# Attention by pairs of heads, and the values product in three rounded parts, in a hybrid layer on one Trainium2 core

## Chip, core and metric

One Trainium2 chip, one core. The metric is the device time of the kernel in microseconds: 351.48 us is the median of three runs before (351.43 to 351.65).

## The reference

A layer for 256 tokens of width 1024 with two branches whose outputs are gated and added. The part that the change touches is the attention branch: eight heads of 128, causal softmax with a relative bias over one block of 256 keys, then the product of probabilities and values, a gate by silu, and a projection.

```python
logit_own = jnp.einsum('bhqd,bhjd->bhqj', qc, k_own) * scale + bias_own
logit_own = jnp.where(dist_own >= 0, logit_own, NEG_INF)
p = jax.nn.softmax(jnp.concatenate([logit_sel, logit_own], axis=-1), axis=-1)
...
o = (jnp.einsum('bhqkj,bhqkjd->bhqd', p_sel, v_sel)
     + jnp.einsum('bhqj,bhjd->bhqd', p_own, v_own))
...
ya = (ya * jax.nn.silu(za)) @ w_att_proj
```

With 256 tokens there is one block, so `sel` contributes nothing. The other branch is an mLSTM of four heads of 256; its input and forget gates (`ig`, `fg`) go through a log-sigmoid, a running sum and a running maximum, and give factors that scale its scores. Everything is float32.

## The kernel before

After a first phase (normalisation and the q and k projections) the kernel runs through 23 chunks of weights, in order: three of values `va` (344 columns), then two halves each of `za`, `qm`, `km`, `att`, `zm`, `vm`, `om`, `ga`, `gm`, `ml`, `out`. Each chunk is four groups of two weight tiles, so there are 92 groups, numbered from 0. A group of `za`, `qm`, `km`, `att` (groups 12 to 43) is 24 matmuls of 256 columns (lines 1006, 1008 and 1009), and its result lies in PSUM until the chunk's four groups are done.

Each weight is used as two rounded parts in TensorE's one-pass float type (F32R in the code): ACT casts the weight to `wh` (line 448), DVE or, for eight groups from 27 on, POOL subtracts to get `wl` (line 452), and TensorE makes three products, high with high, high with low and low with high. These halves are made four groups ahead (`split(g + 4)`, five buffers), so ACT's cast for group g + 4 waits until TensorE has finished group g - 1.

Everything else is hung on group numbers by hand. `at(g, fn)` runs a piece of work in group g after the cast and subtraction; `between(g, fn)` runs it between the cast and the subtraction. On TensorE both come ahead of group g's own matmuls, so what TensorE does there is a burst of small matmuls between two groups. Each engine works its instructions in this order.

Attention before: for head h, in group 10 + h TensorE makes the scores (`att_qk`, lines 604 and 605) and DVE moves them out with the bias; ACT takes the exponential in the same group (`att_exp`); DVE normalises one group later (`att_norm`); TensorE transposes three groups later (`att_PT`, lines 629 to 631) and ACT copies the result to `PT`. `att_av` takes two heads at a time, in groups 18, 20, 21 and 22: per head one plain float32 product of 256 columns (line 642, keys 0 to 127 for all queries) and one of 128 columns (line 644, keys 128 to 255 for the later queries). DVE multiplies with silu(za), ACT and POOL split the result into `yah` and `yal` (lines 649 and 650), which the projection reads from group 36 on.

The gate factors run beside this: `gates_3` to `gates_7`, `gates_T` and `gates_D` at groups 12 to 21. `gates_5` (group 17) ends with ACT making the tile `GE` (line 565) and SP writing a row to memory (line 567); `gates_T` (group 18) transposes `GE` on TensorE (line 587). Tiles that are not in use at the same time share a place (`slot`): `G`, the gate tile, has the place "s6", the bias the place "bias", which the conditioning vector `cbg` takes over in `gate_init` (line 828).

Of the kernel before, what the change touches and what calls it, by code (L numbers as in the profile page):

```python
# [9 lines left out]
F32 = mybir.dt.float32  # L10
F32R = mybir.dt.float32r
AF = mybir.ActivationFunctionType
OP = mybir.AluOpType
# [5 lines left out]
AH, AD = 8, 128  # L19
# [47 lines left out]
def tile_hybrid(ctx: ExitStack, tc: tile.TileContext, x, c, params2, w_row, w_va, ada_mod, ada_gate,  # L67
                w_in, w_att_proj, w_ml_proj, w_out, out):
    nc = tc.nc
# [163 lines left out]
    for j in range(4):  # L233
        n, q = divmod(j, 2)
        nc.tensor.matmul(pc[:, n, q * 256:(q + 1) * 256], pick[:, j:j + 1].to_broadcast([128, 128]), cparts,
                         start=q == 0, stop=q == 1, skip_group_check=True)
# [66 lines left out]
    for step in P1_STEPS:  # L303
        op, k = step[0], int(step[1])
        if op == "L":
            next_loads(k)
        else:
# [4 lines left out]
                 v=lambda k: split_low(k, nc.vector, 1024, NR), g=lambda k: split_low(k, nc.vector, 1024, 1536),  # L312
                 h=lambda k: split_low(k, nc.vector, 1536, NR), G=modulate_low,
                 c=lambda k: modulation_sum(k, 1), k=lambda k: modulation_sum(k, 0),
                 a=modulation_scale, b=modulation_shift, i=lambda k: modulate(k, "i"), j=lambda k: modulate(k, "j"),
                 P=lambda k: mm_row(k, 0), Q=lambda k: mm_row(k, 1, (0, 1)), q=lambda k: mm_row(k, 1, (2,)),
# [28 lines left out]
    C = {}  # L345
# [3 lines left out]
    def done(name, half):  # L349
        return 4 * (C[name, half] + 1)  # L350
# [76 lines left out]
    def slot(tag, shape, dt, name):  # L427
        free(tag)
        return hl.tile(shape, dt, name=name, tag=tag, bufs=1)

    def aux(shape):
        return ps.tile(shape, F32, name="aux", bufs=4)
# [24 lines left out]
    def at(step, fn, *a):  # L457
        hooks.setdefault(step, []).append((fn, a))

    def between(step, fn, *a):  # L460
        hooks_between.setdefault(step, []).append((fn, a))

    T = {}
# [162 lines left out]
    def att_PT(h):  # L626
# [4 lines left out]
        nc.tensor.transpose(pa[:, 256:384], P[:, 128:256], ident)  # L631
        nc.scalar.copy(T["PT"][:, h], pa)

    def att_av(h0):
        va, PT, sza = T["va"], T["PT"], T["za"]
        if "yah" not in T:
            T["yah"] = slot("s1", [128, AH, S], F32R, "yah")
            T["yal"] = slot("s2", [128, AH, S], F32R, "yal")
        pa = aux([128, 2, 256])
        for hh in range(2):  # L640
            h = h0 + hh
            nc.tensor.matmul(pa[:, hh, :], va[:, 0, h * 128:(h + 1) * 128], PT[:, h, 0:256], start=hh == 0,  # L642
                             stop=False, skip_group_check=True)
            nc.tensor.matmul(pa[:, hh, 128:256], va[:, 1, h * 128:(h + 1) * 128], PT[:, h, 256:384], start=False,
                             stop=hh == 1, skip_group_check=True)
        yf = hl.tile([128, 2, 256], F32, name="yf", tag="scr", bufs=2)
        hs = slice(h0, h0 + 2)
        nc.vector.tensor_tensor(yf, pa, sza[:, hs], op=OP.mult)
        nc.scalar.copy(T["yah"][:, hs], yf)
        nc.gpsimd.tensor_tensor(T["yal"][:, hs], yf, T["yah"][:, hs].bitcast(F32), op=OP.subtract)  # L650
# [232 lines left out]
    at(10, gates_2)  # L883
    at(12, qk_T, "k", 1)
    A0 = 10
    for h in range(AH):
        between(A0 + 1 + h, att_norm, h)
        between(A0 + h, att_qk, h)
        hooks_between.setdefault(A0 + 3 + h, []).insert(0, (att_PT, (h,)))
        at(A0 + h, att_exp, h)  # L890
    for step, fn in ((12, gates_3), (14, gates_copy), (15, gates_4), (17, gates_5), (18, gates_6), (18, gates_T),
                     (19, gates_7), (21, gates_D)):
        at(step, fn)
    for nm in ("qm", "km"):
        for hf in range(2):
            s = done(nm, hf)
            for q in range(2):
                at(s + q, lambda i, *a: conv(mmt[i], *a), C[nm, hf], hf, nm, q)
                at(s + q + 1, conv_silu, hf, nm, q)
    for q in range(2):  # L900
        at(done("za", 0) + 2 + 2 * q, att_av, 2 * q)
        at(done("za", 1) + 1 + q, att_av, 4 + 2 * q)
    s = 4 * C["zm", 0]
    for half in range(2):
        at(s + 5 * half, ml_split, half)
        at(s + 5 * half + 3, ml_scores, 2 * half)
        at(s + 5 * half + 4, ml_scores, 2 * half + 1)
    at(4 * C["att", 0] - 10, gate_init)
    gate_left = {}
    for q, nm in enumerate(GSEG):  # L910
        s = 4 * C[nm, 0] - 4
# [164 lines left out]
```

## Time and profile before

| | |
|---|---|
| median of three runs | 351.48 us |
| profiled execution | 351.84 us, its span 350.0 us |
| TensorE (PE) | 344.3 us busy, 98% of the span |
| DVE, ACT, POOL | 247.0, 213.3 and 87.8 us busy |
| granted TensorE clock | 1.000 |
| groups 12 to 27 (attention, most of it) | 83.56 to 139.25 us of the span |

PE is TensorE, PEld its weight loads, DVE the vector engine, ACT the scalar engine, POOL GpSimd, SP the engine that issues most DMAs. A row of a timeline gives start, length, engine, line, operation and what is written and read; in brackets stands how long the engine was idle before and what ended that. A matmul in plain float32 shows as two records. Durations of matmul records overlap, so what one costs is read from start to start, or from the chain of waits, whose pieces do not overlap.

### The profile page before, as it was taken

What the parts mean: (1) busy time and instruction counts of PE and PEld (TensorE: products, weight loads), DVE (VectorE), ACT (ScalarE), POOL (GpSimd) and SP (SyncE); (2) the same over time, 40 slices, a digit from 0 to 9 for tenths busy, and PEclk for the clock granted to TensorE, in tenths of its full rate; (3) what the DMA queues carried; (4) which work ended last, traced back from release to release, by engine and by line L of the source; (5) the groups of instructions that cost most, each with busy time, mean ns of one, the idle gap of its engine ahead of it and who ended that gap; (6) DMA issues with size and microseconds to landing.
All of it is one profiled execution on the core that took longest, in us unless ns stands there. A gap on an engine that the chain in (4) does not pass through costs nothing.

```text
span 350.0 us, 6175 instructions
## 1 busy us (share of the span) xinstructions
PE 344.3 (98%) x2432; PEld 323.1 (92%) x2432; DVE 247.0 (71%) x369; ACT 213.3 (61%) x331; POOL 87.8 (25%) x81
## 2 busy tenths in 40 slices
PE   8999999999999999999999999999999999999996
PEld 7788889999999999999998888888899999999995
DVE  4999996976994437768866693864475775469961
ACT  4768779799777867675646554445646374543510
POOL 4400002942202462555004352000010320452000
PEclk9999999999999999999999999999999999999999
DMA  7999999890671554493874837659119129291011
GB/s 286 416 413 416 415 419 418 223 385 13 197 285 62 161 200 134 151 375 125 322 279 151 330 120 245 237 163 388 51 29 381 72 70 367 107 292 69 2 62 60
DMA packets 23517, 77.79 MB, mean 222 GB/s; under 512 B 3001, under 2 KB 4929, under 8 KB 22849
## 3 DMA queue, kind: packets, MB, share of 16 engines
q1 hardware_dynamic: 23336, 76.87, 59.9%
q10 hardware_dynamic: 152, 0.53, 0.5%
q8 instruction: 19, 0.31, 0.3%
q14 instruction: 10, 0.07, 0.1%
HBM read 76.14 MB, written 1.25 MB: 221 GB/s over the span
## 4 chain that ended last, share of the span: by engine, by line
PE 96%; DMA 2%; DVE 1%; issue 0%; SPq 0%; ACT 0%; DVEq 0%; ACTq 0%
PE mm L1009 15%; PE mm L1006 15%; PE mm L1008 15%; PE pm L198 13%; PE mm L999 8%; PE mm L1000 8%; PE mm L1001 8%; PE mm L992 3%; DMA adat<-in_ada_mod_dram 2%; PE mm L1021 1%; PE aux L642 1%; PE mm L1020 1%; PE mm L1019 1%; PE aux L492 1%; PE aux L604 1%; PE aux L762 1%
## 5 line engine op out<-in xcount | busy, mean ns | idle before, releaser
L452 DVE TENSOR_TENSOR wl<-raw,wh 128x1024 fp32r<-128x1024 f32 (+1 forms) x92 | 118.7, 1302 | 64.1 <-ACT wh L448 64.1
L448 ACT CAST wh<-raw 128x1024 fp32r<-128x1024 f32 (+1 forms) x100 | 100.5, 1015 | 54.2 <-PE mm L1001 26.7
L1006 PE MATMUL mm<-hTh,wh 128*128 128x256 f32 x320 | 90.0, 281 | 0.0
L1008 PE MATMUL mm<-hTl,wh 128*128 128x256 f32 x320 | 88.7, 277 | 0.0
L1009 PE MATMUL mm<-hTh,wl 128*128 128x256 f32 x320 | 88.7, 277 | 0.0
L1006 PEld LDWEIGHTS mm<-hTh,wh 128*128 128x128 f32 x320 | 60.2, 188 | 0.0
L1008 PEld LDWEIGHTS mm<-hTl,wh 128*128 128x128 f32 x320 | 60.2, 188 | 0.0
L1009 PEld LDWEIGHTS mm<-hTh,wl 128*128 128x128 f32 x320 | 60.1, 188 | 0.0
L999 PE MATMUL mm<-wh,hTh 128*128 128x512 f32 (+1 forms) x144 | 53.0, 368 | 0.0
L1000 PE MATMUL mm<-wl,hTh 128*128 128x512 f32 (+1 forms) x144 | 52.6, 365 | 0.0
L1001 PE MATMUL mm<-wh,hTl 128*128 128x512 f32 (+1 forms) x144 | 52.6, 365 | 0.0
L1001 PEld LDWEIGHTS mm<-wh,hTl 128*128 128x128 f32 x144 | 27.0, 188 | 3.8
L999 PEld LDWEIGHTS mm<-wh,hTh 128*128 128x128 f32 x144 | 27.0, 188 | 3.6
L1000 PEld LDWEIGHTS mm<-wl,hTh 128*128 128x128 f32 x144 | 27.1, 188 | 3.5
L452 POOL TENSOR_TENSOR wl<-raw,wh 128x1024 fp32r<-128x1024 f32 x8 | 19.5, 2461 | 18.4 <-ACT wh L448 12.1
L183 ACT CAST wrh<-raw 128x512 fp32r<-128x512 f32 (+1 forms) x24 | 18.2, 761 | 8.0 <-DMA raw<-in_w_row_dram 7.9
L188 DVE TENSOR_TENSOR wrl<-raw,wrh 128x512 fp32r<-128x512 f32 (+1 forms) x26 | 20.3, 807 | 0.5 <-ACT wrh L183 0.5
L198 PE MATMUL pm<-wrh,hTh 128*128 128x512 f32 x64 | 19.9, 392 | 0.8 <-ACT hTh L168 0.8
L198 PE MATMUL pm<-wrh,hTl 128*128 128x512 f32 x64 | 19.8, 391 | 0.0
L198 PE MATMUL pm<-wrl,hTh 128*128 128x512 f32 x64 | 18.7, 391 | 0.0
L1009 PE MATMUL mm<-yah,wl 128*128 128x256 f32 x64 | 17.7, 276 | 0.0
L1006 PE MATMUL mm<-yah,wh 128*128 128x256 f32 x64 | 17.7, 276 | 0.0
(218 smaller groups left out, 659.3 us busy)
## 6 DMA issues: line engine op xcount, KB each, us to landing
raw<-in_w_in_dram SPq DMA_DIRECT2D x32, 1024.0 KB, 5.2
adat<-in_ada_mod_dram SPq DMA_DIRECT2D x16, 512.0 KB, 8.8
raw<-in_w_va_dram SPq DMA_DIRECT2D x6, 688.0 KB, 9.2
raw<-in_ada_gate_dram SPq DMA_DIRECT2D x4, 1024.0 KB, 6.8
raw<-in_w_att_proj_dram SPq DMA_DIRECT2D x4, 1024.0 KB, 4.8
raw<-in_w_ml_proj_dram SPq DMA_DIRECT2D x4, 1024.0 KB, 6.3
raw<-in_w_out_dram SPq DMA_DIRECT2D x4, 1024.0 KB, 6.3
raw<-in_w_row_dram SPq DMA_DIRECT2D x15, 256.0 KB, 8.1
```

Source lines behind the costliest of these rows:

```text
L183: copy(wsp[k][0][:, c0:c1], wrow[k][:, c0:c1])
L188: e.tensor_tensor(l[:, cs], wrow[k][:, cs], h[:, cs].bitcast(F32), op=OP.subtract)
L198: nc.tensor.matmul(pm[ch][:, t], a[:, k, t * 128:(t + 1) * 128], b[:, cs], start=k == 0 and i == 0, stop=k == KT - 1 and i == 2)
L448: nc.scalar.copy(h, w)
L452: e.tensor_tensor(l, w, h.bitcast(F32), op=OP.subtract)
L992: nc.tensor.matmul(mmt[ci][:, t, cs], a, w[:, kk, cs], start=first and i == 0 and c0 == 0 and w is wh, stop=last and i == 1 and c0 > 0, sk ...
L999: nc.tensor.matmul(o, a, wh[:, kk], start=first, stop=False)
L1000: nc.tensor.matmul(o, a, wl[:, kk], start=False, stop=False)
L1001: nc.tensor.matmul(o, b, wh[:, kk], start=False, stop=last)
L1006: nc.tensor.matmul(o, wh[:, kk, cs], sh_[:, k], start=first and i % 2 == 0, stop=False, skip_group_check=True)
L1008: nc.tensor.matmul(o, wh[:, kk, cs], sl_[:, k], start=False, stop=False, skip_group_check=True)
L1009: nc.tensor.matmul(o, wl[:, kk, cs], sh_[:, k], start=False, stop=last and i % 2 == 1, skip_group_check=True)
```

## The change

Three things, in the order of the code.

1. `att_av` is made of three rounded products per head instead of one plain one for the 256-column part. A new function `av_split` makes the parts for two heads: ACT casts the values of the two heads (`vh`, 128x256) and their transposed probabilities (`PTs`, 128x512) and POOL subtracts to get the lower parts. It runs in groups 18 and 20 for the first four heads and in 23 and 24 for the last four. `att_av` then runs for four heads in group 23 and for four in group 27 (before: two each in 18, 20, 21 and 22). The 128-column part stays plain. `PTs` lies in the place of `G` for the first four heads and in that of the bias for the last four; `vh` and `vl` take the places of `P`.
2. Attention runs by pairs of heads: scores of two heads in groups 10, 12, 14 and 16, normalisation of both one group later, transposes of both four groups later (14, 16, 18, 20).
3. `gates_5` moves from group 17 to 16, and `gate_init` from group 26 to 28.

```diff
+    def av_split(h0):
+        if h0 % 4 == 0:
+            T["PTs", h0] = slot("bias" if h0 else "s6", [128, 2, 2, 2, 256], F32R, "PTs")
+        p = T["PTs", h0 // 4 * 4][:, h0 // 2 % 2]
+        vh, vl = (hl.tile([128, 256], F32R, name=nm, tag="P", bufs=4) for nm in ("vh", "vl"))
+        T["vs", h0] = vh, vl
+        for h, l, src in ((vh, vl, T["va"][:, 0, h0 * 128:h0 * 128 + 256]), (p[:, 0], p[:, 1], T["PT"][:, h0:h0 + 2, 0:256])):
+            nc.scalar.copy(h, src)
+            nc.gpsimd.tensor_tensor(l, src, h.bitcast(F32), op=OP.subtract)
+
     def att_av(h0):
...
         pa = aux([128, 2, 256])
+        ps_, (vh, vl) = T["PTs", h0 // 4 * 4][:, h0 // 2 % 2], T["vs", h0]
         for hh in range(2):
             h = h0 + hh
-            nc.tensor.matmul(pa[:, hh, :], va[:, 0, h * 128:(h + 1) * 128], PT[:, h, 0:256], start=hh == 0,
+            nc.tensor.matmul(pa[:, hh, 128:256], va[:, 1, h * 128:(h + 1) * 128], PT[:, h, 256:384], start=hh == 0,
                              stop=False, skip_group_check=True)
-            nc.tensor.matmul(pa[:, hh, 128:256], va[:, 1, h * 128:(h + 1) * 128], PT[:, h, 256:384], start=False,
-                             stop=hh == 1, skip_group_check=True)
+        for hh in range(2):
+            c = slice(hh * 128, hh * 128 + 128)
+            for i, (v, p) in enumerate(((vh, 0), (vh, 1), (vl, 0))):
+                nc.tensor.matmul(pa[:, hh, :], v[:, c], ps_[:, p, hh], start=False, stop=hh == 1 and i == 2,
+                                 skip_group_check=True)
...
     A0 = 10
-    for h in range(AH):
-        between(A0 + 1 + h, att_norm, h)
-        between(A0 + h, att_qk, h)
-        hooks_between.setdefault(A0 + 3 + h, []).insert(0, (att_PT, (h,)))
-        at(A0 + h, att_exp, h)
-    for step, fn in ((12, gates_3), (14, gates_copy), (15, gates_4), (17, gates_5), (18, gates_6), (18, gates_T),
+    for h in range(0, AH, 2):
+        for fn, d in ((att_PT, 4), (att_qk, 0), (att_norm, 1)):
+            for hh in (h, h + 1):
+                between(A0 + h + d, fn, hh)
+        for hh in (h, h + 1):
+            at(A0 + h, att_exp, hh)
+    for i in range(A0 + 4, A0 + AH + 4, 2):
+        hooks_between[i].sort(key=lambda f: f[0] is not att_PT)
+    for step, fn in ((12, gates_3), (14, gates_copy), (15, gates_4), (16, gates_5), (18, gates_6), (18, gates_T),
                      (19, gates_7), (21, gates_D)):
         at(step, fn)
...
-    for q in range(2):
-        at(done("za", 0) + 2 + 2 * q, att_av, 2 * q)
-        at(done("za", 1) + 1 + q, att_av, 4 + 2 * q)
+    s = done("za", 1)
+    for q0, av, splits in ((0, 3, (-2, 0)), (2, 7, (3, 4))):
+        for q in range(2):
+            at(s + splits[q], av_split, 2 * (q0 + q))
+        for q in range(2):
+            at(s + av, att_av, 2 * (q0 + q))
...
-    at(4 * C["att", 0] - 10, gate_init)
+    at(4 * C["att", 0] - 8, gate_init)
```

What this does to the order of instructions is seen at two places. The first is TensorE's burst with the values product for two heads (`aux` is its PSUM tile, `vat` the values). Before, ahead of group 21:

```order
L1009 MATMUL mm<-hTh,wl 128x256
L642 MATMUL aux<-PT,vat 128x256
L644 MATMUL aux<-PT,vat 128x128
L642 MATMUL aux<-PT,vat 128x256
L644 MATMUL aux<-PT,vat 128x128
L1006 MATMUL mm<-hTh,wh 128x256
```

Now, the first of two such pieces that stand ahead of group 23:

```order
L1029 MATMUL mm<-hTh,wl 128x256
L653 MATMUL aux<-PT,vat 128x128 x2
L658 MATMUL aux<-PTs,vh 128x256 x2
L658 MATMUL aux<-PTs,vl 128x256
L658 MATMUL aux<-PTs,vh 128x256 x2
L658 MATMUL aux<-PTs,vl 128x256
L653 MATMUL aux<-PT,vat 128x128 x2
```

Two plain products of 256 columns are gone and six rounded ones stand in their place, behind the two plain ones of 128 columns; the last row begins the next two heads in the same burst.

The second place is POOL's queue from the gate tile (`NM` is the decay tile, made from the gate factors) to the weight halves of `qm`. Before:

```order
L650 TENSOR_TENSOR yal<-yf,yah 128x512
L578 COPY NM<-NM 128x4x128
L581 AFFINE_SELECT NM<-NM 128x4x128 x2
L650 TENSOR_TENSOR yal<-yf,yah 128x512 x3
L452 TENSOR_TENSOR wl<-raw,wh 128x1024 x8
```

Now:

```order
L642 TENSOR_TENSOR vl<-vat,vh 128x256
L642 TENSOR_TENSOR PTs<-PT,PTs 128x512
L452 TENSOR_TENSOR wl<-raw,wh 128x1024
L664 TENSOR_TENSOR yal<-yf,yah 128x512 x2
L642 TENSOR_TENSOR vl<-vat,vh 128x256
L642 TENSOR_TENSOR PTs<-PT,PTs 128x512
L452 TENSOR_TENSOR wl<-raw,wh 128x1024
L642 TENSOR_TENSOR vl<-vat,vh 128x256
L642 TENSOR_TENSOR PTs<-PT,PTs 128x512
L452 TENSOR_TENSOR wl<-raw,wh 128x1024
L664 TENSOR_TENSOR yal<-yf,yah 128x512 x2
L452 TENSOR_TENSOR wl<-raw,wh 128x1024 x5
```

These rows begin with the second of the four splits. The lower halves of groups 27 and 28 now stand ahead of and between the last two splits, and the four parts of `yal` come in two pairs.

## The prediction

> **What bounds the kernel now.** First the page of the profile: busy time by engine, and the shares of the chain that ended last.
>
> ```profile
> span 350.0 us, 6175 instructions
> PE 344.3 (98%) x2432; PEld 323.1 (92%) x2432; DVE 247.0 (71%) x369; ACT 213.3 (61%) x331; POOL 87.8 (25%) x81
> PE 96%; DMA 2%; DVE 1%; issue 0%; SPq 0%; ACT 0%; DVEq 0%; ACTq 0%
> ```
>
> TensorE is busy for 98% of the span and makes up 96% of the chain. So what counts is TensorE's own issue time, plus any wait that appears in it. Work on ACT, DVE and POOL costs nothing until TensorE has to wait for it. Next the chain in order of time, which gives real issue steps (the durations of matmul records overlap). Columns: start, length in us, what.
>
> ```profile
> 105.69 0.24 PE aux L587 x2
> 105.93 0.63 PE aux L642 x2
> ...
> 114.67 0.22 PE aux L644 x2
> ...
> 117.72 0.43 PE aux L642 x2
> ...
> 118.37 0.43 PE aux L642 x2
> ...
> 118.80 0.22 PE aux L644 x2
> ...
> 121.76 0.43 PE aux L642 x2
> ```
>
> Read three things here. One plain float32 product of values with 256 columns (L642) takes 0.43 us, the 128-column one (L644) 0.22 us. After the burst that ends at 118.80 + 0.22 = 119.02 us, the 24 weight matmuls of a group last until 121.76: 2.74 us. After the burst that ends at 114.67 + 0.22 = 114.89 us, the same work lasts until 117.72: 2.83 us. So TensorE has two paces. The timeline shows both without any burst in between:
>
> ```profile
> 83.56 0.36 PE L1006 MATMUL mm<-hTh,wh 128*128 128x256 f32 x1
> 139.25 0.28 PE L1006 MATMUL mm<-hTh,wh 128*128 128x256 f32 x1
> 271.98 0.28 PE L1006 MATMUL mm<-hTh,wh 128*128 128x256 f32 x1
> 274.80 0.28 PE L1006 MATMUL mm<-hTh,wh 128*128 128x256 f32 x1
> 283.99 0.28 PE L1006 MATMUL mm<-hTh,wh 128*128 128x256 f32 x1
> 286.70 0.28 PE L1006 MATMUL mm<-hTh,wh 128*128 128x256 f32 x1
> ```
>
> Rows 3 to 6 are the starts of neighbouring groups of 24 matmuls: 2.82 us apart in the one place (0.118 each), 2.71 to 2.72 us in the other (0.113 each). Rows 1 and 2 are the starts of groups 12 and 28, which enclose most of the attention: 55.69 us.
>
> **The change part by part.** (a) The product. For each of the eight heads a 0.43 us matmul goes and three rounded ones of the same 256 columns come; the 0.22 us matmul stays. The trace has such rounded products inside a burst, in the mLSTM scores:
>
> ```profile
> 191.56 0.72 PE aux L762 x6
> ```
>
> Six in 0.72 us is 0.120 each; in the weight groups they cost 0.113. Three cost 0.34 to 0.36 us, so a head saves 0.07 to 0.09 us and eight heads 0.56 to 0.74 us. I take 0.65.
>
> (b) The gate factors. In group 18's burst TensorE transposes the tile GE, which ACT has only just made:
>
> ```profile
> PEld aux L587 <- ACT GE L565: 0.2, 1, 0.2
> 105.05 0.42 ACT L565 ACTIVATE GE<-G 4x256 f32<-4x256 f32 x1 [0.89 <-DVE st L622]
> 105.31 0.27 PE L630 MATMUL aux<-ident,P 128*128 128x128 f32 x1
> 105.42 0.27 PE L631 MATMUL aux<-ident,P 128*128 128x128 f32 x1
> 105.62 0.31 PE L587 MATMUL aux<-ident,GE 36*128 36x36 f32 x2
> ```
>
> L630 to L631 is 0.11 us, L631 to L587 0.20: 0.09 lost. The product right behind took 0.63 instead of 0.43 (the chain above), another 0.20, which I can't split into wait and refill. With the factors made in group 16, some 3.7 us sooner, GE is long there. Gain between 0.1 and 0.3; I take 0.25.
>
> (c) Fewer bursts. Attention work stood between the groups fifteen times from group 7 to 22; in pairs it stands there ten times (before groups 7, 8, 10, 12, 14, 16, 18, 20, 23, 27). A burst followed by the quick pace costs 2.74 - 2.72 = 0.02 us, one followed by the slow pace 2.83 - 2.72 = 0.11. Five fewer: 0.1 to 0.55; I take 0.1 and treat the pace by itself.
>
> A ceiling follows from groups 12 to 28: 16 groups x 2.72 = 43.52, five score pairs and eight value pairs of 0.65 = 8.45, 24 transposes x 0.11 = 2.64, gate transposes 0.24, together 54.85 of the 55.69 us. So some 0.85 us of waits, refills and slow pace lie in this stretch, and the change can gain at most 0.74 + 0.85 = 1.6 us.
>
> (d) The splits on ACT and POOL. ACT gets four casts of 128x256 and four of 128x512, POOL four subtractions of each size. Nearest rows:
>
> ```profile
> L452 POOL TENSOR_TENSOR wl<-raw,wh 128x1024 fp32r<-128x1024 f32 x8 | 19.5, 2461 | 18.4 <-ACT wh L448 12.1 <-PE mm L1009 6.3
> L650 POOL TENSOR_TENSOR yal<-yf,yah 128x512 fp32r<-128x512 f32 x4 | 5.2, 1306 | 27.4 <-ACT yah L649 27.4
> L750 POOL TENSOR_TENSOR qms<-qmT,qms x2: 2392/2884/3377, 186.7 to 202.4; 128x1024 fp32r<-128x1024 f32 x2
> L448 ACT CAST wh<-raw 128x1024 fp32r<-128x1024 f32 x88 | 91.4, 1048 | 51.6 <-PE mm L1001 24.2 <-PE mm L1008 21.1 <-issue 1.5
> L632 ACT COPY PT<-aux 128x384 f32<-128x384 f32 x8 | 3.8, 474 | 0.0
> L649 ACT CAST yah<-yf 128x512 fp32r<-128x512 f32 x4 | 2.5, 616 | 4.9 <-DVE yf L648 4.9
> ```
>
> Per pair of heads ACT works 0.35 + 0.62 = about 1 us more, POOL 0.7 + 1.31 = 2.0 us (0.35 and 0.7 are estimates for 256 columns, from the 0.47 of 384 on ACT and from half of 1.31 on POOL). ACT writes a weight group's upper half four groups (11 us) ahead, so 1 us is covered; the cover ends where POOL must finish before TensorE reads. The tight place is the second half. Count from t0, when group 22 ends. ACT comes late, since in group 21 it loads a table and makes the decay tile:
>
> ```profile
> 118.75 1.28 ACT L595 ACT_TABLE_LOAD   x1
> ...
> 122.54 0.39 ACT L596 ACTIVATE NM<-NM,gc 128x128 f32<-128x128 f32 x1
> ```
>
> That is 4.2 us behind a 1.0 us cast that waits for group 20's end (t0 - 5.4); two more casts end at about t0 + 1.7. Then POOL has, in order: group 27's lower half 2.46, two lower halves of the attention output 2 x 1.31, one value and probability split 2.0, group 28's lower half 2.46, the last split 2.0: 11.5 us, done at t0 + 13.2. TensorE comes to the last lower half after two products (2 x 1.1), four groups (10.9), one product (1.1) and three matmuls (0.55): t0 + 14.8. Slack 1.6 us; no wait. The first half is easier: its splits start in groups 18 and 20 and are read at 23. What is queued on POOL behind the last split is group 31's lower half, needed four groups later. ACT's DMA of the conditioning vector moves two groups back, behind the last products; it landed 3.7 us after issue at 138.4, and its first reader starts at 154.6:
>
> ```profile
> L828 ACTq DMA_DIRECT2D cbg<-in_c_dram x1: 365/365/365, 138.4 to 138.4; - x1
> DMA to landing us min/median/max: 3.7/3.7/3.7
> L832 DVE CUSTOM_DVE_ANT_0 raw<-raw,cbg,prm x8: 1274/1279/2321, 154.6 to 226.1; 128x1024 f32<-128x1024 f32 x8
> ```
>
> Two groups (5.4 us) later is still over 7 us early. SP issues the factors' small write one group sooner, past the weight loads of that group only; ACT's first probability cast waits for that write, made some 5 us before. Both at nothing.
>
> Sum: 0.65 + 0.25 + 0.1 = 1.0 us. The profiled execution took 351.84 us (span 350.0 and 1.84 around it), 0.36 above the median of 351.48. Off its own time that is 350.8; the terms are issue times that every execution pays, so I take them off the median: **350.5 us**.
>
> **The rivals.** *The slow pace catches on behind the last burst (slower).* The pace after a burst stays as it is until something disturbs it: in the rows at 271.98 and 274.80 it stayed slow over a border between groups with no burst there. Before, the last attention burst stood ahead of group 22 and happened to be followed by the quick pace. Now the last stands ahead of group 27, with another form of matmul at its end, and 17 groups of 24 follow before the shape changes at group 44. If it catches there, it costs 17 x 0.11 = 1.8 us, and the time is 350.5 + 1.8 = 352.3. It turns to slower than before from 10 of these groups on (1.0 / 0.107). For it: of the two bursts of products quoted first, one went slow and one quick. Against: over the whole trace slow is the rarer one, about one burst in three, and a single disturbance ends it. Chance 0.22.
>
> *POOL is late for the last split.* A POOL subtraction of 1024 elements has taken 2.39 to 3.38 us here. At 3.38, with the others stretched by the same 1.4, the 11.5 us become 16 and TensorE waits up to 3.0 us; at the 2.88 median of that row they become 13.5, a wait of 0.4 us. What stretches them is DVE working beside POOL:
>
> ```profile
> 89.49 0.73 POOL L544 TENSOR_TENSOR G<-G 4x256 f32<-4x256 f32 x1 [8.53 <-ACT wh L448]
> 89.57 0.80 DVE L623 TENSOR_SCALAR P<-P,st 128x256 f32<-128x256 f32 x1
> 93.01 0.35 DVE L623 TENSOR_SCALAR P<-P,st 128x256 f32<-128x256 f32 x1
> 123.51 1.31 POOL L650 TENSOR_TENSOR yal<-yf,yah 128x512 fp32r<-128x512 f32 x1 [4.87 <-ACT yah L649]
> 124.42 1.49 DVE L452 TENSOR_TENSOR wl<-raw,wh 128x1024 fp32r<-128x1024 f32 x1 [3.83 <-ACT wh L448]
> ...
> L452 DVE TENSOR_TENSOR wl<-raw,wh x92: 861/1224/3408, 50.4 to 334.3; 128x1024 fp32r<-128x1024 f32 x80, 128x688 fp32r<-128x688 f32 x12
> ```
>
> The same DVE instruction takes 0.35 us alone and 0.80 beside POOL, and one with two inputs 1.49 against a median of 1.22; POOL's own kept its 1.31. So DVE mostly pays, and POOL's 1.6 us of slack should hold. If POOL were held for the whole of each of the two DVE subtractions of groups 29 and 30 (1.22 each), it would come 0.8 us late: 351.3. Chance of a late POOL 0.13, at 350.9 to 351.3 and seldom more. The Trainium skill, page "SBUF — State Buffer", section "SBUF: two separate sides", says that the port pair which DVE and GpSimd share is an exclusive lock, the loser blocked for the whole instruction; that is the 351.3 case, and it speaks against moving work to POOL. The first two rows above agree with it (DVE as the loser), the last two only in part: 1.49 us is less than the 0.40 us left of POOL's instruction plus a full 1.22.
>
> *Only the product counts.* The bursts become longer and the pace after the short ones (groups 12 to 26, 15 groups) may be slow in half of them: 7 x 0.107 = 0.75 us given back, or GE's gap is a refill that stays. Time 350.9 to 351.3. For it: three short stretches were slow before. Chance 0.17.
>
> **How the numbers follow.** Chances: forecast 0.48 (350.0 to 351.0), product only 0.17, late POOL 0.13, slow pace 0.22. The range reaches from the ceiling, 351.48 - 1.6 = 349.9, to the slow pace held throughout, 352.3. A measurement of this kernel can tell about 0.2% (0.7 us) from no change: faster is under 350.8, slower over 352.2. Faster takes nearly all of the forecast and some of the product-only case: 0.52. Slower is two thirds of the slow pace and a POOL worse than bounded: 0.17. Same is the rest: 0.31.
>
> **What would show it.** Right: three rounded products in 0.34 to 0.36 us in place of 0.43; no gap ahead of the gate transposes; ten bursts; groups 28 to 43 at 2.72 us. Wrong: groups 28 to 43 at 2.82; TensorE idle ahead of the last products with POOL as what ended it; a new wait of TensorE for ACT or DVE in groups 12 to 22, where the pairs ask two tiles of each at once.

## The result and the profile after

The changed kernel takes 353.61 us (median of four runs, 352.92 to 354.01), the kernel before 351.46 us beside it (351.32 to 351.65). The ratio is 1.006, 95% interval 1.0044 to 1.0076: slower by some 2 us. The forecast was 350.5 us with a range up to 352.3, so both the sign and the range were wrong.

The page of the changed kernel: span, busy time by engine, share of the chain that ended last.

```profile
span 351.6 us, 6213 instructions
PE 345.9 (98%) x2440; PEld 324.1 (92%) x2440; DVE 248.7 (71%) x369; ACT 216.8 (62%) x339; POOL 101.0 (29%) x89
PE 98%; ACT 1%; POOL 0%; DVE 0%; issue 0%; POOLq 0%
```

The profiled execution took 353.35 us. The span grew by 1.6 us, and so did TensorE's busy time (344.3 to 345.9), although TensorE has less to do than before. It is not waiting for a neighbour: DVE and POOL are 0% of the chain, and ACT's 1% lies in its first 7 us. Its own instructions take longer. The timeline shows where (first matmuls of groups 7, 28, 29, 30 and 44):

```profile
69.34 0.40 PE L1019 MATMUL mm<-wh,hTh 128*128 128x344 f32 x1
...
139.09 0.28 PE L1026 MATMUL mm<-hTh,wh 128*128 128x256 f32 x1
...
141.92 0.28 PE L1026 MATMUL mm<-hTh,wh 128*128 128x256 f32 x1
...
144.75 0.28 PE L1026 MATMUL mm<-hTh,wh 128*128 128x256 f32 x1
...
184.32 0.40 PE L1019 MATMUL mm<-wh,hTh 128*128 128x512 f32 x1
```

Groups 28 and 29 take 2.83 us each, with no burst between them, and groups 28 to 43 together 45.23 us: 16 x 2.827. Before, the same 16 groups took 43.52 us: 16 x 2.72, from 139.25 to 182.77. The starts of groups 7 and 44 in the timeline of the kernel before:

```profile
69.52 0.40 PE L999 MATMUL mm<-wh,hTh 128*128 128x344 f32 x1
...
182.77 0.40 PE L999 MATMUL mm<-wh,hTh 128*128 128x512 f32 x1
```

The difference is 1.71 us, more than the whole growth of the span, in a place where the change adds nothing to TensorE. In the records TensorE is in the slow pace (0.1178 us from matmul to matmul in place of 0.1133) from group 18 without a break to group 43, in 26 groups. Before, only groups 12, 13 and 20 of those from 12 to 43 were slow. 26 x 0.107 is 2.8 us.

The products themselves went as forecast. Chain of waits of the changed kernel, start, length, what; L653 are the plain 128-column products, L658 the rounded ones:

```profile
120.50 0.45 PE aux L653 x4
120.94 0.71 PE aux L658 x6
...
135.28 0.44 PE aux L653 x4
135.72 0.71 PE aux L658 x6
```

Six rounded products in 0.71 us are 0.118 each; three replace a plain one of 0.43, so a head saves 0.08 and eight heads 0.62 us. POOL was in time too: in its timeline the last split (L642) ends at 132.99 + 1.30 = 134.29 us, and TensorE's first product that can read it starts at 135.72. The rows also show a split before it, and DVE's subtraction beside the last one:

```profile
126.98 0.75 POOL L642 TENSOR_TENSOR vl<-vat,vh 128x256 fp32r<-128x256 f32 x1
...
128.95 2.39 POOL L452 TENSOR_TENSOR wl<-raw,wh 128x1024 fp32r<-128x1024 f32 x1
...
129.95 2.47 DVE L452 TENSOR_TENSOR wl<-raw,wh 128x1024 fp32r<-128x1024 f32 x1
...
131.30 1.73 POOL L642 TENSOR_TENSOR vl<-vat,vh 128x256 fp32r<-128x256 f32 x1
132.99 1.30 POOL L642 TENSOR_TENSOR PTs<-PT,PTs 128x512 fp32r<-128x512 f32 x1
```

The gate transposes did not get cheaper. In the timeline the factors `GE` are ready at 104.05 + 0.42 = 104.47, half a microsecond ahead of the last attention transpose, and yet the step from L631 to L587 is 0.21 us, as before:

```profile
104.05 0.42 ACT L565 ACTIVATE GE<-G 4x256 f32<-4x256 f32 x1 [0.56 <-DVE st L622]
...
104.98 0.27 PE L631 MATMUL aux<-ident,P 128*128 128x128 f32 x1
105.19 0.31 PE L587 MATMUL aux<-ident,GE 36*128 36x36 f32 x2
105.42 0.39 PE L1026 MATMUL mm<-hTh,wh 128*128 128x256 f32 x1
```

The waits of TensorE's weight loads put these 0.2 us to no engine ("issue"), where before they named ACT:

```profile
PEld aux L587 <- issue: 0.2, 1, 0.2
```

So the question for the experiments: is the pace the whole loss, what sets it off, and can the gain be had without it?

One table serves all of them. It gives, from the starts of the groups' first matmuls in each profile, the time from group 7 to 28 (attention) and from 28 to 44 (weight groups alone), and the groups from 12 to 43 that ran slow, by the mean step between their matmuls. The stage behind, from the start of group 44 to that of 91, took 139.0 to 139.3 us in every kernel (the 23 chunks and 92 groups named at the start leave out the two halves of `out`; with them there are 25 chunks and 100 groups, 0 to 99). Group 7 starts between 68.9 and 70.0 us, differently in each execution, so spans are not compared beyond that. Each row is a single execution. For e1, e2, v1 and v2 that execution took 0.8 to 1.0 us more than the median of the kernel's runs, so what is slow in these rows need not be slow in every run.

| kernel | 7 to 28 | 28 to 44 | sum | slow groups |
|---|---|---|---|---|
| before | 69.73 | 43.52 | 113.25 | 12, 13, 20 |
| changed | 69.75 | 45.23 | 114.98 | 18 to 43 |
| plain products last (e1) | 69.21 | 43.72 | 112.93 | 18 to 22 |
| disturbance at 32 (e2) | 69.75 | 44.43 | 114.18 | 18 to 31 |
| rounded products alone (e3) | 69.71 | 45.23 | 114.94 | 12, 13, 18, 19, 23 to 43 |
| before, with a burst at 28 (e4) | 70.89 | 45.23 | 116.12 | 12, 13, 20, 28 to 43 |
| pairs and gates alone (p1) | 69.38 | 43.51 | 112.89 | none |
| gates first (v1) | 68.98 | 44.93 | 113.91 | 20 to 22, 32 to 43 |
| one transpose at 18 (v2) | 68.76 | 44.07 | 112.83 | none |
| POOL shifted everywhere (v3) | 68.75 | 45.02 | 113.77 | 40 to 43 |
| wide matmuls (w1) | 69.62 | 43.52 | 113.14 | none |
| POOL at 33 alone (v4) | 68.76 | 43.52 | 112.28 | none |

### The profile page after: what moved, and what is told of

It is laid out like the page before. It is cut to its first block, busy times and chain, and to the rows that moved or that the text cites. A ratio compares the mean times of both kernels' runs of the same rounds, so it can differ in the third digit from the quotient of the medians.

```text
span 351.6 us, 6213 instructions
## 1 busy us (share of the span) xinstructions
PE 345.9 (98%) x2440; PEld 324.1 (92%) x2440; DVE 248.7 (71%) x369; ACT 216.8 (62%) x339; POOL 101.0 (29%) x89
## 3 DMA queue, kind: packets, MB, share of 16 engines
HBM read 76.14 MB, written 1.25 MB: 220 GB/s over the span
## 4 chain that ended last, share of the span: by engine, by line
PE 98%; ACT 1%; POOL 0%; DVE 0%; issue 0%; POOLq 0%
PE mm L1026 15%; PE mm L1028 15%; PE mm L1029 15%; PE pm L198 13%; PE mm L1019 8%; PE mm L1020 8%; PE mm L1021 8%; PE mm L1012 3%; PE xps L263 1%; PE mm L1039 1%; PE mm L1041 1%; PE mm L1040 1%; PE aux L492 1%; PE aux L604 1%; PE aux L776 1%; PE aux L658 1%
```

## The experiments

**The plain products last.** The same work in another order inside each values burst: rounded products first, the plain 128-column ones behind them.

```diff
@@ att_av, changed kernel
-            nc.tensor.matmul(pa[:, hh, 128:256], va[:, 1, h * 128:(h + 1) * 128], PT[:, h, 256:384], start=hh == 0,
...
             for i, (v, p) in enumerate(((vh, 0), (vh, 1), (vl, 0))):
...
+            nc.tensor.matmul(pa[:, hh, 128:256], va[:, 1, h * 128:(h + 1) * 128], PT[:, h, 256:384], start=False,
+                             stop=hh == 1, skip_group_check=True)
```

> Changed kernel, but in each values burst the two plain 128-column products stand last, behind the six rounded ones; nothing else moves. Theory pace (TensorE keeps the pace with which a burst lets it go, until something disturbs it; the new burst, which ends in six rounded matmuls, lets it go slow): the burst now ends as before the change, after which groups 18, 21 and 22 of the kernel before were quick and 20 slow; groups 28 to 43 at 2.72 us in place of 2.83, time 351.5 to 352.0 (353.6 less 1.7 or a little more). Theory neighbours (what DVE, ACT and POOL do beside it, or where the new tiles lie, slows TensorE from group 18 to 43): no change, 353.4 to 353.8.

Measured: 350.93 us against 351.27 of the kernel before; ratio 0.9993 (0.9981 to 1.0004). Against the changed kernel that is some 2.5 us less, each set against the kernel before that ran beside it, from an edit that removes no instruction. Chain of waits around the last burst, and then, from the timeline, the starts of groups 28 and 29:

```profile
135.40 0.71 PE aux L654 x6
136.11 0.44 PE aux L658 x4
```

```profile
139.13 0.28 PE L1026 MATMUL mm<-hTh,wh 128*128 128x256 f32 x1
...
141.85 0.28 PE L1026 MATMUL mm<-hTh,wh 128*128 128x256 f32 x1
```

The products cost what they did (L654 now the rounded, L658 the plain ones), and the group behind takes 2.72 us again. All splits on ACT and POOL are still there, so the load on the neighbours is not the cause.

**A disturbance at group 32.** The changed kernel and four transposes of the identity ahead of group 32, read by nobody.

```diff
+    def stir(n):
+        pa = aux([128, 128])
+        for _ in range(n):
+            nc.tensor.transpose(pa, ident, ident)
...
+    at(32, stir, 4)
```

> Changed kernel with four extra transposes of the identity into a spare PSUM tile ahead of group 32 (0.44 us of TensorE, read by nobody). Theory pace: groups 28 to 31 stay slow at 2.83 us, groups 32 to 43 go quick at 2.72 with odds of about two in three: 12 x 0.107 = 1.3 less, 0.44 more, time 352.7. Theory neighbours: groups 32 to 43 as slow as 28 to 31, time 354.0.

Measured: 351.99 us, ratio 1.0027 (1.0015 to 1.0039): more work on TensorE, and some 1.4 us less than the changed kernel, each set against the kernel before that ran beside it. Timeline, starts of group 31, of the transposes, and of groups 32, 33 and 34:

```profile
148.02 0.28 PE L1032 MATMUL mm<-hTh,wh 128*128 128x256 f32 x1
...
150.85 0.60 PE L881 MATMUL aux<-ident 128*128 128x128 f32 x4
...
151.20 0.37 PE L1032 MATMUL mm<-hTh,wh 128*128 128x256 f32 x1
...
154.05 0.28 PE L1032 MATMUL mm<-hTh,wh 128*128 128x256 f32 x1
...
156.77 0.28 PE L1032 MATMUL mm<-hTh,wh 128*128 128x256 f32 x1
```

From 148.02 to the transposes are 2.83 us, group 33 takes 2.72. The pace turns exactly at the disturbance. Groups 33 to 43 have the same data and the same work beside them as in the changed kernel, where they were slow. So the pace is no property of these groups; it lasts until something breaks it.

**The rounded products alone.** The kernel before with the splits and the rounded products at their new places; heads one by one and `gates_5` at 17, as before.

```diff
@@ kernel before
+    def av_split(h0):
...
+            for i, (v, p) in enumerate(((vh, 0), (vh, 1), (vl, 0))):
...
-            at(done("za", 0) + 2 + 2 * q, att_av, 2 * q)
-            at(done("za", 1) + 1 + q, att_av, 4 + 2 * q)
+            at(s + av, att_av, 2 * (q0 + q))
```

> Kernel before with the rounded values product alone (splits, four heads in groups 23 and 27, conditioning vector at 28); heads are still worked one by one and the gate factors stay in group 17. Theory pace: the same two bursts as in the changed kernel, so groups 23 to 43 slow, 21 x 0.107 = 2.2 lost and 0.65 won: 353.0. If the pairs are what makes it slow: 350.8 to 351.0.

Measured: 352.88 us, ratio 1.0048 (1.0033 to 1.0063). Groups 20 to 22 are quick; from the first values burst, ahead of group 23, all are slow. So the pairs of heads are not needed for the loss.

**A burst in the kernel before.** Nothing of the change, only two plain and six rounded products at group 28, on tiles that are there anyway, read by nobody.

```diff
@@ kernel before
+    def extra_burst():
+        pa = aux([128, 2, 256])
+        for hh in range(2):
+            nc.tensor.matmul(pa[:, hh, 128:256], ident, ident, start=hh == 0, stop=False, skip_group_check=True)
+        for hh in range(2):
+            for i in range(3):
+                nc.tensor.matmul(pa[:, hh, :], hTh[:, i, hh * 128:hh * 128 + 128], hTl[:, i], start=False,
...
+    at(28, extra_burst)
```

> Kernel before with one extra burst ahead of group 28: two plain 128-column products and six rounded 256-column ones on tiles that are there anyway, into a spare PSUM tile (about 1.15 us of TensorE, read by nobody). No work is added to ACT, DVE or POOL. Theory pace: quick up to group 27, slow at 2.83 us in groups 28 to 43: 351.5 + 1.15 + 1.7 = 354.3. Theory neighbours: groups 28 to 43 quick, 352.6.

Measured: 354.84 us, ratio 1.0100 (1.0083 to 1.0117). Group 27 takes 2.72 us ahead of the burst, groups 28 to 43 take 45.23, as in the changed kernel. The burst itself costs 1.2 us, its wake 1.7.

**Pairs and gates alone.** The kernel before with heads in pairs and `gates_5` at 16; products as before.

```diff
@@ kernel before
-    for h in range(AH):
-        between(A0 + 1 + h, att_norm, h)
...
+    for h in range(0, AH, 2):
+        for fn, d in ((att_PT, 4), (att_qk, 0), (att_norm, 1)):
...
-    for step, fn in ((12, gates_3), (14, gates_copy), (15, gates_4), (17, gates_5), (18, gates_6), (18, gates_T),
+    for step, fn in ((12, gates_3), (14, gates_copy), (15, gates_4), (16, gates_5), (18, gates_6), (18, gates_T),
```

> Kernel before with the pairs of heads and the gate factors in group 16 alone; the values product stays plain and in groups 18, 20, 21 and 22. By the steps of the prediction: five bursts fewer is not reached here (11 in place of 15), 0.1; the gate wait 0.25 if it was a wait of TensorE for ACT, nothing if the 0.10 us ahead of the 36-row transposes is their own cost (the changed kernel still shows it). Time 350.9 in the first case, 351.2 in the second, plus or minus 0.3 for the pace of groups 18 to 21.

Measured: 351.07 us, ratio 0.9990 (0.9977 to 1.0003). The attention stage is 0.35 us shorter than before. Of this 0.25 us is that groups 12, 13 and 20 were slow before and are quick here (behind a burst the 23 steps of a group take 2.79 us at the slow pace and 2.71 at the quick one, three times 0.08); 0.10 is left for the fewer bursts, eleven in place of fifteen. Nothing is left for the gates: `GE` is ready at 104.31 here, L631 starts at 104.85 and L587 at 105.05, 0.20 us again.

**Maps of what throws the pace.** The kernel before with different bursts ahead of groups 24 to 42, none of which is read; the time means nothing, the pace of the group behind each burst does. The first map has a burst ahead of every second group, the second ahead of every group.

```diff
@@ kernel before
+    def burst(plain, rounded, turns, wide):
...
+            nc.tensor.transpose(pa[:, 0, 0:128], ident, ident)
...
+            nc.tensor.matmul(pa[:, 1, 0:128], ident, ident, start=True, stop=True, skip_group_check=True)
...
+            nc.tensor.matmul(pa[:, i % 2], hTh[:, i % 8, 0:128], hTl[:, i % 8], start=True, stop=True, skip_group_check=True)
...
+            nc.tensor.matmul(pa, hTh[:, 0, 0:128], hTl[:, 0:2], start=True, stop=True, skip_group_check=True)
...
+        at(s, burst, *what)
```

> Kernel before with a small extra burst into a spare PSUM tile ahead of each second group from 24 to 42 (read by nobody): 24 six rounded matmuls; 26 two plain 128-column ones and six rounded; 28 six rounded; 30 two plain; 32 two plain and six rounded; 34 four transposes; 36 two plain and three rounded; 38 one transpose; 40 two plain and one rounded; 42 one rounded of 512 columns. Theory form (plain float32 work throws the pace anew; if rounded matmuls of the burst follow it directly they lock it slow, if the group's own follow it mostly goes quick; rounded work alone changes nothing): group 24 quick, 26 and 28 slow, 30 quick, 32 slow, 34 mostly quick, 36 slow, 38 mostly quick, 40 open, 42 as 40. Theory dice (each burst throws anew, one in three slow, whatever its form): slow and quick spread over 26, 30, 32, 34, 36, 38, 40 without regard to form.

> The kernel before, with extra work of TensorE alone ahead of every weight group from 24 to 42; its results are read by nobody. In order from group 24: wide, 4 transposes, 6 rounded, wide, 6 rounded, 4 transposes, 2 plain, wide, 3 rounded, wide, 3 rounded, 4 transposes, 2 plain + 6 rounded, wide, 2 plain, 4 transposes, 2 plain, wide, 6 rounded (wide: one 512-column rounded matmul; rounded: 256 columns; plain: 128 columns). The time itself (about 20 us more than before) decides nothing; the pace of the group behind each does: 0.1133 us per matmul is quick, 0.1178 slow. Theory 'the form in front decides': each form gives one pace at all its places: 6 rounded slow at all four, wide and transposes quick at all eleven, 2 plain one and the same pace at all three. Rival 'a throw of which the form only sets the chance': at least one of the forms shows both paces; I expect that of 2 plain and 3 rounded, and 6 rounded slow at all four.

Measured: 359.27 us and 360.93 us, one run each. Timeline of the second map: a 512-column matmul (L874), the first and last matmul of group 27; six rounded ones (L872), the first and last of group 28.

```profile
137.60 0.39 PE L874 MATMUL aux<-hTl,hTh 128*128 128x512 f32 x1
137.83 0.28 PE L1020 MATMUL mm<-hTh,wh 128*128 128x256 f32 x1
...
140.44 0.28 PE L1023 MATMUL mm<-hTh,wl 128*128 128x256 f32 x1
140.55 0.88 PE L872 MATMUL aux<-hTl,hTh 128*128 128x256 f32 x6
141.27 0.28 PE L1020 MATMUL mm<-hTh,wh 128*128 128x256 f32 x1
...
143.98 0.28 PE L1023 MATMUL mm<-hTh,wl 128*128 128x256 f32 x1
```

The same 23 steps take 2.61 us behind the one and 2.71 us behind the other. All places of both maps:

| last in the burst | pace behind it, first map | second map |
|---|---|---|
| one 512-column | quick (1 of 1) | quick (6 of 6) |
| six rounded, alone or behind two plain | slow (4 of 4) | slow (4 of 4) |
| three rounded | quick (1 of 1, behind two plain) | slow (2 of 2) |
| one rounded behind two plain | slow (1 of 1) | |
| two plain 128-column | slow (1 of 1) | slow (3 of 3) |
| four transposes | quick (1 of 1) | quick (3 of 4) |
| one transpose | slow (1 of 1) | |

The first map's theory of forms was wrong at three places (24, 30, 36); besides, group 38 was slow where mostly quick was expected, and 40 and 42, expected to go alike, did not. In the second map a 512-column matmul and a run of six rounded ones gave one pace each, as the theory had it. Four transposes gave both, against it, and against the rival's guess, which was that two plain and three rounded products would. Two plain products, slow in all four places here, stand at the end of bursts that were followed by the quick pace in the first experiment. So for the other forms a rule was not found. Nor does the order of instructions alone decide: four transposes stand ahead of group 72 in every kernel, in code that no run changed, and groups 72 to 74 were slow in eleven of the fourteen profiles and quick in three (e2, e3 and the second map).

**A wide matmul behind the bursts.** The changed kernel with one 512-column rounded matmul, read by nobody, at the end of the bursts ahead of groups 18, 20, 23 and 27.

```diff
+    def wide():
+        pa = aux([128, 2, 256])
+        nc.tensor.matmul(pa, hTh[:, 0, 0:128], hTl[:, 0:2], start=True, stop=True, skip_group_check=True)
...
+    for i in (18, 20, 23, 27):
+        at(i, wide)
```

> The changed kernel with one more matmul at the end of the bursts ahead of groups 18, 20, 23 and 27: a rounded product of 512 columns, read by nobody, 0.235 us each. Nothing else is moved. Theory 'the pace is the loss, and a 512-column matmul ahead of the groups restores the quick one': groups 18 to 43 at 2.72 us, so 26 x 0.107 - 4 x 0.235 = 1.84 us less than the changed kernel's 353.61: 351.8. Rival 'something else holds TensorE back there, or the wide matmul does nothing in this kernel': groups 18 to 43 stay at 2.826 and the four matmuls are paid: 354.5.

Measured: 351.09 us, ratio 0.9995 (0.9987 to 1.0004). All of groups 12 to 43 are quick; from group 7 to 44 it takes 113.14 us where the changed kernel takes 114.98: the 1.84 us expected. The median came 0.7 below the expected 351.8; in its profile 0.47 of that is the start of group 7 (68.87 against 69.34), which neither kernel touches. Four useless matmuls bring back what the change had lost.

**Towards a faster version.** First, on top of the first experiment, the gate transposes at the head of group 18's burst.

```diff
@@ plain products last
-    for step, fn in ((12, gates_3), (14, gates_copy), (15, gates_4), (16, gates_5), (18, gates_6), (18, gates_T),
+    for step, fn in ((12, gates_3), (14, gates_copy), (15, gates_4), (16, gates_5), (18, gates_6),
...
+    hooks_between[18].insert(0, (gates_T, ()))
```

> The kernel with plain products last (e1), and the transposes of the gate factors at the head of group 18's burst, ahead of the six transposes of probabilities, in place of behind them. Theory pace: in e1 groups 18 to 22 are slow behind the gate transposes, 5 x 0.107 = 0.54; with the ordinary transposes last they go quick with odds of two in three: 350.4. If they stay slow: 350.9. If pace has to do with what the other engines do in groups 18 to 22: 350.9.

Measured: 351.83 us, ratio 1.0001 (0.9983 to 1.0020), its runs spread from 350.22 to 353.44. In its profile groups 18 and 19 are quick, but 20 to 22 slow, and from 32 to 43 it is slow again, behind a wait of TensorE of 0.05 us at the border and no burst at all. So the pace can turn at a short wait as well. The spread of the runs suggests that it does not in every execution; only one was profiled. Then, instead of that, a single transpose of the identity behind the gate transposes:

```diff
@@ plain products last
+    at(18, stir, 1)
```

> e1 with one extra transpose of the identity behind the gate transposes of group 18 (0.11 us, read by nobody). Theory pace: groups 18 to 22 quick with odds of two in three, 350.9 - 0.54 + 0.11 = 350.5; if slow, 351.0.

Measured: 351.05 us, ratio 0.9996 (0.9984 to 1.0007). No group is slow in its profile, but 0.55 us are lost between groups 28 and 44: TensorE waits 0.26 us ahead of group 32 and 0.10 ahead of 36, and the first step behind each wait is 0.08 longer. The timeline shows POOL, DVE and TensorE (last matmul of group 31, first of group 32):

```profile
143.89 2.40 POOL L452 TENSOR_TENSOR wl<-raw,wh 128x1024 fp32r<-128x1024 f32 x1
...
144.48 2.89 DVE L452 TENSOR_TENSOR wl<-raw,wh 128x1024 fp32r<-128x1024 f32 x1
147.30 2.42 DVE L696 SCALAR_TENSOR_TENSOR qmT<-mm,prm,qmT 128x255 f32<-128x255 f32 x6
...
149.48 0.28 PE L1035 MATMUL mm<-hTh,wl 128*128 128x256 f32 x1
149.86 0.36 PE L1032 MATMUL mm<-hTh,wh 128*128 128x256 f32 x1
```

In the waits of TensorE's weight loads no engine is named for it:

```profile
PEld mm L1032 <- issue: 0.3, 1, 0.3
```

DVE's subtraction, whose median was 1.22 us before, takes 2.89 beside POOL's; the convolution that reads the finished PSUM tiles ends late, at 149.72, and group 32 starts 0.14 us behind it and 0.26 late. That it waited for DVE is a reading of the order, and the next two runs test it. The other traces bear it out. TensorE waits at five borders from 28 to 40 in all profiles: 32 and 36 here, 36 in e1, 32 in v1 and 40 in v3 below. Each time the group starts 0.14 to 0.15 us behind the end of DVE's convolution; at the borders without a wait that distance is 0.25 us or more. The gates-first version (v1), DVE's convolution and the start of group 32:

```profile
147.05 2.42 DVE L696 SCALAR_TENSOR_TENSOR qmT<-mm,prm,qmT 128x255 f32<-128x255 f32 x6
...
149.61 0.35 PE L1027 MATMUL mm<-hTh,wh 128*128 128x256 f32 x1
```

First, POOL takes the lower halves one group later nearly everywhere (33, 37, 41 for 32, 36, 40):

```diff
@@ one transpose at 18
-            pool_lo.update((done(nm, hf) + 3, done(nm, hf) + 4))
+            pool_lo.update((done(nm, hf) + 3, done(nm, hf) + (5 if (nm, hf) != ("qm", 0) else 4)))
```

> The changed kernel with the plain 128-column products last in each values burst, one transpose of the identity behind the gate transposes of group 18 (as in the version before this one), and POOL taking the lower halves of weight groups 33, 37, 41 ... in place of 32, 36, 40 ... after the first. Theory 'DVE was held by POOL': with POOL's subtraction moved away from DVE's of the neighbouring group, DVE's 2.89 us subtraction ahead of group 32 is back near 1.22, TensorE's wait of 0.26 us ahead of group 32 is gone and with it the chance to fall into the slow pace there: 350.7 us, where the version before it gave 351.05. Rival 'the wait has another cause, or it only moves': TensorE still waits at a border between groups 31 and 36, and the time stays at 351.0 or above.

Measured: 352.36 us, ratio 1.0021 (1.0011 to 1.0030). The wait at 32 is gone, but it has moved, as the rival said. The timeline ahead of group 40, with group 40's first matmul, where the profile now names DVE's convolution:

```profile
161.62 6.21 POOL L452 TENSOR_TENSOR wl<-raw,wh 128x1024 fp32r<-128x1024 f32 x2 [5.89 <-ACT wh L448]
...
162.53 3.04 DVE L452 TENSOR_TENSOR wl<-raw,wh 128x1024 fp32r<-128x1024 f32 x1 [0.31 <-ACT wh L448]
...
172.15 0.36 PE L1032 MATMUL mm<-yah,wh 128*128 128x256 f32 x1 [0.83 <-DVE kmT L696]
```

TensorE loses 1.0 us there, and the four groups behind are slow. Then group 32's half alone goes to DVE and group 33's to POOL, with all others as in the change:

```diff
@@ one transpose at 18
+    pool_lo.symmetric_difference_update((32, 33))
```

> The changed kernel with the plain 128-column products last and one transpose of the identity behind the gate transposes of group 18, and POOL taking the lower half of group 33 in place of group 32, all its other groups as in the changed kernel. Theory 'DVE was held by POOL ahead of group 32': the wait of 0.26 us there goes and none comes at group 40, since groups 35, 36, 39 and 40 are shared out as before: groups 18 to 43 quick, 350.7 us. Rival 'the wait only moves': TensorE waits at another border between groups 28 and 44, 351.0 or more.

Measured: 350.35 us against 351.34 of the kernel before; ratio 0.9973 (0.9962 to 0.9984). This one is faster than both, than the kernel before by 0.3%. Its timeline, with the starts of groups 7, 28 and 44 and DVE's work ahead of group 32:

```profile
68.94 0.40 PE L1026 MATMUL mm<-wh,hTh 128*128 128x344 f32 x1
...
137.70 0.28 PE L1033 MATMUL mm<-hTh,wh 128*128 128x256 f32 x1
...
145.47 2.43 DVE L697 SCALAR_TENSOR_TENSOR qmT<-mm,prm,qmT 128x255 f32<-128x255 f32 x6 [1.67 <-ACT qmT L691]
147.82 1.22 DVE L453 TENSOR_TENSOR wl<-raw,wh 128x1024 fp32r<-128x1024 f32 x1
...
181.22 0.40 PE L1026 MATMUL mm<-wh,hTh 128*128 128x512 f32 x1
```

DVE's convolution ends at 147.90, ahead of group 32's start at 148.58, its subtraction takes 1.22 us again, no border between 28 and 44 has a wait, and the stage is back at 43.52 us. It is the change plus three edits: plain products last, one idle transpose, and one group's half exchanged between POOL and DVE.

## Why the prediction was wrong

**The step that failed** is the pace. Part (c) put the fewer bursts at 0.1 us and treated "the pace by itself" at nothing, and the rival that names it, the slow pace caught behind the last burst, got a chance of 0.22. That rival's mechanism is what happened, and 28 to 43 slow is the sign that the text gave for being wrong. Two things in it were mis-sized. Its chance: it rested on slow being the rarer pace "over the whole trace", one burst in three, but the bursts counted there end in other forms; the text saw that the new burst ends in another form and drew nothing from it. A run of six rounded 256-column matmuls ahead of such a group was followed by the slow pace at every place that these runs have (the changed kernel, e2, e3, e4 and both maps: 15 places, six of them behind a quick group), and the change puts just that at the end of its last two bursts. And its length: 17 groups were counted, from 27 on; in fact the pace was caught at group 18, behind the gate transposes, and lasted 26 groups, 2.8 us in place of 1.8.

**(a) The product** was right: 0.118 us a rounded product, 0.62 us won where 0.65 was taken.

**(b) The gate factors** were wrong. The 0.20 us ahead of L587 are not a wait for ACT: `GE` was 0.5 us early in the changed kernel and the step stayed, also with pairs and gates alone. Nor is it tied to the attention transposes, since in v1 it is 0.21 us behind a weight matmul. So it belongs to the step into these 36-row transposes; why it is so long no run shows. The 0.20 us that the product right behind had lost did not come back either: with pairs and gates alone its two records start 0.32 us apart, as before (0.22 for the next head). In the changed kernel, with no products there, the first step of group 18 is 0.23 us, where 0.20 is usual behind transposes. 0.25 was taken, 0 was measured.

**(c) Fewer bursts**: 0.10 us with pairs and gates alone, for four bursts fewer, where 0.1 was taken for five; and 0.25 on top because three groups happened to be quick there that were slow before.

**(d) The splits at nothing** were right in the changed kernel: POOL's last split ended 135.72 - 134.29 = 1.4 us ahead of its reader, where a slack of 1.6 was worked out. The rival of a late POOL fell. But the cover is thin. Some 4 x 0.107 = 0.4 us of it come from the slow pace of the four groups between. And POOL was held, as that rival feared: the last `vl` took 1.73 us where the same instruction took 0.75 one split earlier, and DVE's subtraction beside it ended at 129.95 + 2.47 = 132.42, 1.1 us after `vl` had started. Here both paid, DVE 1.25 us (2.47 for 1.22) and POOL 1.0, where the prediction had DVE pay nearly all. With one transpose at 18 and TensorE quick, DVE was held beside POOL and made TensorE late at group 32 (0.26 us). In the changed kernel, at the slow pace, the same subtraction took 1.95 us and nothing waited.

In the row of 2.89 us, POOL's subtraction ends at 143.89 + 2.40 = 146.29 us, and from there to the end of DVE's are 1.08 us, not far from its own 1.22: it stood still while POOL worked. In the changed kernel's rows above the rest is 1.08 as well (128.95 + 2.39 to 129.95 + 2.47), and in those of the prediction it is 1.09 (123.51 + 1.31 to 124.42 + 1.49). The Trainium skill, page "SBUF — State Buffer", section "SBUF: two separate sides", calls this an exclusive lock for the whole instruction. All three rows agree with it; the prediction took the 1.49 us for only partly in agreement because it set a full 1.22 behind POOL's end.

**The sum** held, then, under a condition that the text did not give the weight it has. In the last version, quick throughout, the stage from 7 to 28 is 0.97 us shorter than before (0.62 of products and the 0.35 that pairs and gates alone gave), and the median 0.99 us lower; the forecast had 1.0, with 0.25 of it put to the gates and not to the three groups that were slow before. That the total comes out is in part luck, and the match to 0.01 too: the last version also has one transpose more and one burst less than pairs and gates alone. In the changed kernel the same gain is used up within the stage by ten slow groups (10 x 0.107 = 1.07), and sixteen more add 1.71.

**What stays open** is what decides the pace in general. The same form of burst gave both paces at different places, waits of 0.05 and 1.0 us were followed by the slow one, waits of 0.10 and 0.26 by the quick one, and the same code went both ways at group 72. The runs show that the pace is the loss, two forms that set it reliably, and that it lasts; not the mechanism.

## What to carry to other kernels

Where TensorE runs back to back through many equal matmuls, compare the length of equal groups without a burst before and after a change: a few per cent there, times hundreds of matmuls, outweigh what is saved in a burst. What stands last ahead of such a stretch is worth trying in another order, or with one wide matmul behind it, since the pace that it leaves stayed until the next disturbance in every profile here. And a wait that is hidden while TensorE is slow has to be costed again at the pace hoped for.

## What the hardware did that was not expected

A stream of 256-column rounded matmuls, each with its own weight load, runs at one of two steady paces, 0.1133 or 0.1178 us a matmul, at a granted clock of 1.0 in both, and keeps it: the changed kernel stayed slow for 26 groups, over three bursts. The loads show a trace of it. Weight loads of the changed kernel between groups 28 and 44, in groups by line (the three products of each weight, mean ns at the end):

```profile
L1026 PEld LDWEIGHTS mm<-hTh,wh 128*128 128x128 f32 x63 | 12.1, 192 | 0.0
L1028 PEld LDWEIGHTS mm<-hTl,wh 128*128 128x128 f32 x64 | 12.0, 188 | 0.0
L1029 PEld LDWEIGHTS mm<-hTh,wl 128*128 128x128 f32 x64 | 12.0, 188 | 0.0
```

In the slow pace one load in three, that of the first product, takes 192 ns. In the kernel before, quick in this stretch, all three take 188; the load of the first product there:

```profile
L1006 PEld LDWEIGHTS mm<-hTh,wh 128*128 128x128 f32 x64 | 12.0, 188 | 0.0
```

Whether the longer load is the cause or another sign of the same thing no run tells.
